# Groups of small matmuls ranked forty numbers ahead, and a norm's sums traced later, in a two-layer trunk

## The chip, the cores and the metric

The kernel runs on one core of one Trainium2 chip. The metric is the device time of one execution in microseconds. TensorE (PE in the profile, PEld for its weight loads) multiplies, VectorE (DVE) and ScalarE (ACT) do elementwise work, GpSimd (POOL) adds squares and clears tiles, SyncE (SP) issues the weight DMAs.

## The reference

A trunk of two layers on x of 512 tokens by 1024 features, all in fp32.

```python
for l in range(DEPTH):                       # DEPTH = 2
    h = rms_norm(x, attn_norm[l])
    if l % 2 == 0:  mix = hgrn_rwkv_mixer(h, ...)     # 4 HGRN heads, 8 RWKV heads, then @ w_out
    else:           mix = moba_mixer(h, ...)          # 8 attention heads, then @ w_o
    x = x + mix
    h = rms_norm(x, mlp_norm[l])
    x = x + square(relu(h @ w_up[l])) @ w_down[l]     # d_ff = 4096
    ple = rms_norm(p[l] @ ple_proj[l], ple_norm[l])   # p: the second input, 256 features
    x = x + ple * sigmoid(x @ ple_gate[l])
```

`rms_norm` divides by the root of the mean square over the features.

## The kernel before

Features lie on the partitions and the 512 tokens on the free axis, so x is eight tiles of 128 x 512. A large product (`gemm`, `mm3`, L243 to L259) splits weights and activations into a high part (fp32r) and a rest, and does three 512-column matmuls for each 128 x 128 block of weights (L244, L245, L246). Weights come in pieces of 128 x 512 (`wnext`): a DMA, ACT's cast to `whi` (L236), DVE's rest `wlo` (L237). The results stand in PSUM rings: `pj` and `pmh` with two banks each, `pmr` with four.

**Layer 0's mixer** has two streams of small work beside the large projections. The HGRN heads h = 0 to 3 (`hgrn`) use `pmh`. The RWKV head pairs (`pre`, `p1`, `p2`, `p3`, `tail`) use `pmr`. The small jobs are groups: four or so matmuls of 64 or 128 columns, or transposes, into one bank, which an evacuation follows. L664 (`half4`) are f16 groups of the inversion of a triangular matrix in `p2`, L519 (`four`) another, L710 and L711 are fp32 products of `p3`; an fp32 matmul shows as two passes in the trace. Steps are traced for each h in the order A F H B O C: A and C are runs of RWKV work, F the three projections of the HGRN head, H the HGRN head, B the projections of the next RWKV head, O an eighth of the output projection (`out_piece`). L803 is the first matmul group of an HGRN head and L896 its last.

**The order on each engine** is made when the program is built. Every traced instruction gets the next number. The scheduler plays the program through with its own costs and gives each engine, whenever it is free, the ready instruction with the lowest number. Each engine then works strictly in this order and waits for data where the scheduler was too early. `tc.high_priority(offset=n)` lowers the numbers inside by n; on leaving, the numbering goes on from where it was, so that instructions inside use up no numbers outside. `run` (L786) and the RWKV projections use `OFS` = 300. In the numbers of this program, head after head starts 314 later.

**The norms.** `NormAcc` (L306) squares each x tile on ACT (L313) and sums the squares on GpSimd (L319) into one tile `acc`, of which there is one buffer for all norms. `Stats.add` (L289) then sums over partitions by matmuls with ones (L291), `rs` takes the reciprocal root on DVE in 12 small steps (L300, L264 to L269), and `norm_rows` spreads the result over the partitions with transposes (L334) and an ACT copy (`rb`, L343). `later` (L1010) holds steps back: `flush` is called at each evacuation of the output projection of layer 1 and of the up products, and an entry of count n is traced at the (n+1)th call.

**Layer 0's MLP** gets its norm from code at the end (L1302): eight `add` calls, then `later_norm(st, 3, 1)`. **Layer 1's MLP** gets it inside `proj_out`: each evacuation adds to x (L1085), then `post` makes the scaled split (L280, L281) and traces the square and the sum; `later_norm(st, 2)` follows. **The second input** (`ple`, L1026) is projected, summed by its own `NormAcc`, and finished by `rows` (the root; L1047) and `finish` (transposes, then eight DVE steps, L1052). It is needed only in the gate after the MLP. In layer 1 `rows` comes at the 6th flush, in the output projection, and `finish` at the 9th, the first of the up product; in layer 0 `finish` comes at the 9th as well. The up products keep their PSUM banks until the norm's row is there: the first four use `pmr`, the next `pj`.

Of the kernel before, what the change touches and what calls it, by code (L numbers as in the profile page):

```python
# [12 lines left out]
F32 = mybir.dt.float32  # L13
# [16 lines left out]
FD = (3, 5)  # L30
# [4 lines left out]
OFS = 300  # L35
NWARM = 9
# [149 lines left out]
def trunk(ctx, tc, wts, xT, pT, vecs, lora, cst, lev, seg, rope, gain, out, upto="all", dbg=None, mode=None):  # L186
# [97 lines left out]
    class Stats:  # L284
# [4 lines left out]
        def add(self, sq, rhs):  # L289
            for j in range(NJ):  # L290
                T.matmul(self.ps[:, j * self.cols:(j + 1) * self.cols], sq[:, j * P:(j + 1) * P], rhs,  # L291
                         start=(self.i == 0 and j == 0), stop=(self.i == self.n - 1),
                         skip_group_check=True)
            self.i += 1
# [31 lines left out]
    def bcast_rows(rt, cols, pool, tag):  # L326
        ps = pool.tile([P, S], F32, name=tag)
        if cols > 1:
            full = nrm.tile([P, S], F32, name="bc")
            V.tensor_copy(full.rearrange("p (c w) -> p c w", w=P // cols),  # L330
                          rt[:, :, None].to_broadcast([P, NJ * cols, P // cols]))
        for j in range(NJ):
            lhs = full[:, j * P:(j + 1) * P] if cols > 1 else rt[:, j:j + 1].to_broadcast([P, P])
            T.transpose(ps[:, j * P:(j + 1) * P], lhs, ident)  # L334
        return ps
# [28 lines left out]
    def layer0_mixer(actp):  # L364
# [223 lines left out]
        def p1(hp, g):  # L588
            lw, bh, kh, ar, rh_, bo, dl, v, y = pre_[hp]
            gs = slice(g * 256, g * 256 + 256)  # L590
            NA, KA, TOK = NAs[g], KAs, []
            un[hp, g] = (NA, TOK)

            for n, (src, dst) in enumerate(((bh, NA), (kh, KA))):
                for h in range(2):
                    A.copy(BH[hs[h], n, :, hs[h]], src[hs[h], gs].rearrange("p (c t) -> p c t", t=64))
                ps = pmr.tile([P, S], F32, name="pmr")
                for c_ in range(4):
                    o = g * 256 + c_ * 64
                    T.matmul(ps[:, c_ * P:c_ * P + P].rearrange("p (x t) -> p x t", x=2), BH[:, n, c_, :],  # L600
                             ar[:, :, o:o + 64], start=True, stop=True)
                pv = ps.rearrange("p (a c x t) -> p a c x t", a=2, c=2, x=2)
                for h in range(2):
                    for c_ in range(2):
                        V.tensor_tensor(dst[hs[c_], :, h, :, hs[c_]], pv[hs[h], :, c_, :, :],
                                        tri[hs[h], None, :, :].to_broadcast([64, 2, 2, 64]), op=OP.mult)
                yield
            for a in range(2):
                j = 2 * g + a
                js = slice(j * P, j * P + P)  # L610

                ps = pmr.tile([P, S], F32, name="pmr")
                for n, src in enumerate((ar[:, 0, :], v, bh, kh)):
                    T.transpose(ps[:, n * P:n * P + P], src[:, js], ident)
# [9 lines left out]
            for i, (a, h) in enumerate(pk):  # L624
                T.matmul(ps[:, i * 64:i * 64 + 64], KA[:, a, h, 0, :], TOK[a][:, 1, hs[h]], start=True, stop=True)
# [4 lines left out]
            for i, (a, h) in enumerate(pk):  # L630
                T.matmul(ps[hs[h], a * P:a * P + P], TOK[a][:, 1, hs[h]], KA[:, a, h, 1, :], start=True, stop=True)
            A.copy(y[:, gs], ps[:, :256])
            yield

        def p2(hp, g):
# [11 lines left out]
            for l in range(1, 6):  # L647
# [27 lines left out]
            for i, (a, h) in enumerate(pk):  # L675
                T.matmul(ps[:, i * P:i * P + P], NA[:, a, h, 0, :], tt[:, i, :], start=True, stop=False)
                T.matmul(ps[:, i * P:i * P + P], id16, id16, start=False, stop=True)
# [4 lines left out]
            for i in range(4):  # L682
                T.matmul(ps[:, i * P:i * P + P], er[:, i, :], XT[:, i, :], start=True, stop=False)
                T.matmul(ps[:, i * P:i * P + P], id16, XT[:, i, :], start=False, stop=True)
# [4 lines left out]
            for i, (a, h) in enumerate(pk):  # L689
                T.matmul(ps[:, i * P:i * P + P].rearrange("p (x f) -> p x f", x=2), tt[:, i, :],  # L690
                         TOK[a][:, 0::2, hs[h]], start=True, stop=True)
# [6 lines left out]
        def p3(hp, g):  # L698
# [5 lines left out]
            for a in range(2):  # L704
# [3 lines left out]
                for c_ in range(2):  # L708
                    o = ps[:, 256 + c_ * P:256 + c_ * P + P]
                    T.matmul(o, bz[:, 0, c_, :], MU[:, a, 1, :], start=True, stop=False)  # L710
                    T.matmul(o, bz[:, 1, c_, :], TOK[a][:, 1, :], start=False, stop=True)  # L711
# [11 lines left out]
            def inner():  # L723
                ps = pmr.tile([P, S], F32, name="pmr")
                for i, (a, h) in enumerate(pk):
                    T.matmul(ps[hs[h], a * P:a * P + P], MU[:, a, 0, hs[h]], NA[:, a, h, 1, :], start=True, stop=True)
# [3 lines left out]
                for i, (a, h) in enumerate(pk):  # L730
                    T.matmul(ps[hs[h], a * P:a * P + P], MU[:, a, 1, hs[h]], NA[:, a, h, 1, :], start=True, stop=True)
# [20 lines left out]
            for c_ in range(f, 4):  # L752
                ch = 4 * g + c_
                T.matmul(ps[:, c_ * 64:c_ * 64 + 64], SB[:, ch, :], rh_[:, ch * 64:ch * 64 + 64], start=True, stop=True)
# [43 lines left out]
        def hgrn(h, q, ff, iv, gproj):  # L798
# [3 lines left out]
            for j in range(NJ):  # L802
                T.transpose(ps[:, j * P:j * P + P], iv[:, j * P:j * P + P], ident)  # L803
# [25 lines left out]
            for j in range(NJ):  # L829
                js = slice(j * P, j * P + P)  # L830
                T.matmul(ps[:, js], ks[:, js], d[:, js], start=True, stop=True)
            V.copy_predicated(at, m8[:, 13, None, :].to_broadcast([P, NJ, P]), j4(ps))
            for l in range(2, 7):
# [15 lines left out]
                for j in range(NJ):  # L849
                    js = slice(j * P, j * P + P)  # L850
                    T.matmul(ps[:, j * 64:j * 64 + 64], ks[:, js], qs[:, j * 64:j * 64 + 64], start=True, stop=True)
# [15 lines left out]
            for j in range(3):  # L867
                T.transpose(ps[:, j * P:j * P + P], d[:, j * P:j * P + P], ident)
# [3 lines left out]
            for j in range(3):  # L872
                T.matmul(ps[:, j * P:j * P + P], kt[:, j * P:j * P + P], vt[:, j, :], start=True, stop=True)
# [6 lines left out]
            for j in range(NJ):  # L880
                js = slice(j * P, j * P + P)
                T.matmul(ps[:, js], at[:, j, :], vt[:, j, :], start=True, stop=(j == 0))
                if j:
                    T.matmul(ps[:, js], q[:, js], st_[:, j * P - P:j * P], start=False, stop=True)
# [10 lines left out]
            for j in range(NJ):  # L895
                T.transpose(ps[:, j * P:j * P + P], ot[:, j * P:j * P + P], ident)  # L896
# [128 lines left out]

    def ple(l, plp):  # L1026
# [12 lines left out]
        def body():  # L1039
# [3 lines left out]
            later.append([FD[l] + 3, finish])  # L1043
# [303 lines left out]
```

## Time and profile before

| | us |
|---|---|
| median of 3 runs | 1511.21 |
| lowest and highest | 1510.91, 1512.28 |
| the profiled execution | 1511.89 |
| its span, first to last instruction | 1510.1 |
| TensorE busy in the span | 1478.1 |
| layer 0's mixer, from the start to the MLP | 0 to about 450 |
| layer 0's MLP and gate | about 450 to 865 |
| layer 1's attention | about 865 to 1089 |
| layer 1's output projection (second half) | 1086 to 1106 |
| layer 1's MLP and gate | 1106 to 1510 |

All times in the text are in microseconds from the first instruction of the profiled execution. A matmul's duration includes its way through the array, so the time that one costs TensorE is read from the start of one to the start of the next.

### The profile page before, as it was taken

The page shows a single profiled execution, that of the slowest core. Times are in us where ns is not written, and L with a number is a line of the kernel's source. Part 1 is how long each engine was busy: PE and PEld are TensorE (multiplying, and loading weights), DVE is VectorE, ACT ScalarE, POOL GpSimd, SP SyncE. Part 2 cuts the span into 40 slices and gives each one's busy share as a digit, 9 for nine tenths or more (in the row PEclk, how much of TensorE's full clock was granted, in tenths as well). Part 3 has the DMA queues.
Part 4 walks back from the last instruction along what each step waited for, and adds up shares of the span by engine and source line. Part 5 has one row for each costly group of instructions (what it writes and reads, how often), then busy time and mean ns, then how long its engine had stood idle before and what let it go on. Part 6 is the DMA issues. An engine that isn't in the chain of part 4 may idle for free.

```text
span 1510.1 us, 20495 instructions
## 1 busy us (share of the span) xinstructions
PE 1478.1 (98%) x7546; PEld 1191.3 (79%) x7546; DVE 937.6 (62%) x1835; ACT 663.1 (44%) x1269; POOL 138.4 (9%) x133
## 2 busy tenths in 40 slices
PE   8899999999989999999999999999999999999998
PEld 6678777777667888888888888777778888888887
DVE  6878797687785664444446648377575444445463
ACT  4675545554446433333334534455634333333342
POOL 4121220310205000000000200000220000000000
PEclk9999999999999999999999999999999999999999
DMA  5110111211123233333333432221123333333331
GB/s 179 56 36 22 55 50 39 66 29 47 39 91 106 90 98 98 98 98 98 98 95 98 124 118 84 77 63 50 56 80 95 95 101 98 98 96 93 98 98 70
DMA packets 67109, 123.88 MB, mean 82 GB/s; under 512 B 7632, under 2 KB 8016, under 8 KB 67008
## 3 DMA queue, kind: packets, MB, share of 16 engines
q1 hardware_dynamic: 65376, 118.57, 25.6%
q10 hardware_dynamic: 1152, 2.43, 0.5%
q0 software_dynamic: 480, 1.57, 0.3%
q8 instruction: 59, 0.97, 0.3%
q14 instruction: 42, 0.34, 0.1%
HBM read 120.45 MB, written 2.10 MB: 81 GB/s over the span
## 4 chain that ended last, share of the span: by engine, by line
PE 87%; DVE 7%; ACT 3%; issue 2%; DMA 1%; POOL 1%; SPq 0%; DVEq 0%; ACTq 0%; POOLq 0%
PE pj L244 20%; PE pj L246 20%; PE pj L245 20%; PE pmr L1273 1%; PE pmr L245 1%; PE pmr L1249 1%; PE pmr L246 1%; PE pmr L244 1%; PE pj L1176 1%; PE pmr L1176 1%; PE pj L1178 1%; PE pmr L1177 1%; PE pmr L1178 1%; PE pj L1177 1%; PE pmh L1176 1%
## 5 line engine op out<-in xcount | busy, mean ns | idle before, releaser
L236 ACT CAST whi<-wr 128x512 fp32r<-128x512 f32 x428 | 265.0, 621 | 549.2 <-PE pj L245 421.9
L237 DVE TENSOR_TENSOR wlo<-wr,whi 128x512 fp32r<-128x512 f32 x428 | 312.5, 733 | 197.6 <-ACT whi L236 193.6
L244 PE MATMUL pj<-act,whi 128*128 128x512 f32 (+1 forms) x856 | 338.1, 396 | 1.2 <-DVE h L935 1.0
L245 PE MATMUL pj<-act,whi 128*128 128x512 f32 (+1 forms) x856 | 336.8, 394 | 0.0
L246 PE MATMUL pj<-act,wlo 128*128 128x512 f32 (+1 forms) x856 | 335.7, 393 | 0.5 <-DVE wlo L237 0.5
L244 PE MATMUL pj<-hid,whi 128*128 128x512 f32 x512 | 199.2, 389 | 0.0
L245 PE MATMUL pj<-hid,whi 128*128 128x512 f32 x512 | 199.2, 389 | 0.0
L246 PE MATMUL pj<-hid,wlo 128*128 128x512 f32 x512 | 199.2, 389 | 0.0
L244 PEld LDWEIGHTS pj<-act,whi 128*128 128x128 f32 x856 | 161.1, 188 | 34.4 <-ACT k L491 1.4
L246 PEld LDWEIGHTS pj<-act,wlo 128*128 128x128 f32 x856 | 161.2, 188 | 32.5 <-DVE wlo L237 1.5
L245 PEld LDWEIGHTS pj<-act,whi 128*128 128x128 f32 x856 | 161.2, 188 | 31.1 <-issue 1.5
L1115 DVE TENSOR_TENSOR x<-x,pj 128x512 f32<-128x512 f32 x128 | 88.0, 688 | 80.6 <-PE pj L246 80.2
L245 PEld LDWEIGHTS pj<-hid,whi 128*128 128x128 f32 x512 | 96.1, 188 | 20.0
L244 PEld LDWEIGHTS pj<-hid,whi 128*128 128x128 f32 x512 | 96.1, 188 | 19.9
L246 PEld LDWEIGHTS pj<-hid,wlo 128*128 128x128 f32 x512 | 96.1, 188 | 19.9
L319 POOL TENSOR_TENSOR acc<-acc,xsq 128x512 f32<-128x512 f32 x35 | 48.7, 1393 | 628.8 <-ACT xsq L313 616.0
L1104 DVE SCALAR_TENSOR_TENSOR r<-pj,rb 128x512 f32<-128x512 f32 x56 | 38.7, 691 | 84.0 <-PE pj L246 84.0
L278 DVE TENSOR_TENSOR hid<-r,hid 128x512 fp32r<-128x512 f32 x64 | 44.3, 691 | 41.5 <-ACT hid L277 41.4
L1105 ACT ACTIVATE r<-r 128x512 f32<-128x512 f32 x64 | 40.5, 632 | 21.6 <-DVE r L1104 21.5
L277 ACT CAST hid<-r 128x512 fp32r<-128x512 f32 x64 | 39.8, 621 | 1.9
L280 ACT ACTIVATE act<-x,vec 128x512 fp32r<-128x512 f32 x32 | 22.9, 720 | 29.4 <-DVE x L1133 12.7
L244 PE MATMUL pj<-os,whi 128*128 128x512 f32 x64 | 28.3, 445 | 4.4 <-DVE x L946 2.8
(387 smaller groups left out, 2225.8 us busy)
## 6 DMA issues: line engine op xcount, KB each, us to landing
wr<-in_wts_dram SPq DMA_DIRECT2D x428, 256.0 KB, 2.7
x<-in_xT_dram SPq DMA_DIRECT2D x8, 256.0 KB, 6.3
sr<-in_wts_dram SPq DMA_DIRECT2D x8, 256.0 KB, 5.3
out_dram<-x SPq DMA_DIRECT2D x7, 256.0 KB, 2.0
r<-in_pT_dram ACTq DMA_DIRECT2D x4, 256.0 KB, 3.0
lw<-in_lora_dram POOLq DMA_DIRECT2D x4, 192.0 KB, 3.1
tq<-in_rope_dram ACTq DMA_DIRECT2D x1, 512.0 KB, 6.7
tk<-in_rope_dram ACTq DMA_DIRECT2D x1, 512.0 KB, 7.6
```

The lines of the kernel that those rows point to most:

```text
L236: A.copy(hi, raw)
L237: V.tensor_sub(lo, raw, hi.bitcast(F32))
L244: T.matmul(ps, wh, xh, start=first, stop=False)
L245: T.matmul(ps, wh, xl, start=False, stop=False)
L246: T.matmul(ps, wl, xh, start=False, stop=last)
L277: A.copy(h, src)
L278: V.tensor_sub(l, src, h.bitcast(F32))
L319: G.tensor_add(self.t, self.t, sq)
L1104: V.scalar_tensor_tensor(r, q, 0.0, nf[0], op0=OP.max, op1=OP.mult)
L1105: A.activation(r, r, AF.Square)
L1115: V.tensor_add(x[k], x[k], ps)
L1176: T.matmul(ps[j], xh, wh, start=k == 0, stop=False)
```

## The change

A context `tight()` is `tc.high_priority(offset=40)`. It is put around the small groups: in `Stats.add`, in `bcast_rows`, and at 20 places in the mixer, of which two are shown. DVE's, ACT's and GpSimd's instructions are not inside it. Layer 1's MLP norm is taken out of `proj_out` into `rows_norm`, which layer 0 uses too, and `finish` moves by six flushes in both layers.

```diff
+TIGHT = 40
+    def tight():
+        return tc.high_priority(offset=TIGHT)
     class Stats:
         def add(self, sq, rhs):
-            for j in range(NJ):
-                T.matmul(...)
+            with tight():
+                for j in range(NJ):
+                    T.matmul(...)
     def bcast_rows(rt, cols, pool, tag):
-        for j in range(NJ):
-            T.transpose(...)
+        with tight():
+            for j in range(NJ):
+                T.transpose(...)
         def four(lhs, rhs):
             ps = pmr.tile([P, S], F32, name="pmr")
-            for i in range(4):
-                T.matmul(ps[:, i * P:i * P + P], lhs(i), rhs(i), start=True, stop=True)
+            with tight():
+                for i in range(4):
+                    T.matmul(ps[:, i * P:i * P + P], lhs(i), rhs(i), start=True, stop=True)
...
                 def half4(lhs, rhs):
-                    for i in range(4):
-                        T.matmul(pv[:, i], lhs[:, i, :], rhs[:, i], start=True, stop=True)
+                    with tight():
+                        for i in range(4):
+                            T.matmul(pv[:, i], lhs[:, i, :], rhs[:, i], start=True, stop=True)
...
+    def rows_norm():
+        st = NormAcc(lambda: tmp.tile([P, S], F32, name="xsq"))
+        for k in range(8):
+            st.add(x[k])
+        return later_norm(st, 3, 1)
     def ple(l, plp):
             later.append([FD[l], rows])
-            later.append([FD[l] + 3, finish])
+            later.append([FD[l] + 9, finish])
     def proj_out(name, acts, l):
-        st, xg = NormAcc(lambda: tmp.tile([P, S], F32, name="xsq")), []
+        xg = []
                 V.tensor_add(x[k], x[k], ps)
-                post(k, st, act, "act", vcol(f"mn{l}", k), xg)
+                xg.append(split(act, x[k], "act", vcol(f"mn{l}", k)))
-        return st, xg
+        return xg
...
-        st = NormAcc(lambda: tmp.tile([P, S], F32, name="xsq"))
-        for k in range(8):
-            st.add(x[k])
-        nf = later_norm(st, ND[0] + 1, 1)
+        nf = rows_norm()
...
-        st, xg = proj_out("o", o, 1)
-        xs = mlp(1, later_norm(st, ND[1]), xg)
+        xg = proj_out("o", o, 1)
+        xs = mlp(1, rows_norm(), xg)
```

## Rows read from the trace of the kernel before

**Rows 1.** Part 1 of the page: busy time, share of the span, instructions.

```profile
PE 1478.1 (98%) x7546; PEld 1191.3 (79%) x7546; DVE 937.6 (62%) x1835; ACT 663.1 (44%) x1269; POOL 138.4 (9%) x133
```

**Rows 2.** Stretches: bounds, length, busy of PE PEld DVE ACT POOL, clock, DMA.

```profile
20.00:385.00 365.00, 353.27 (x2429) 277.64 (x2427) 278.68 (x658) 194.53 (x435) 64.34 (x68) 1.00 0.15 46
385.00:440.00 55.00, 47.73 (x313) 36.69 (x313) 44.88 (x106) 25.46 (x52) 11.01 (x9) 0.99 0.21 63
455.00:490.00 35.00, 33.05 (x149) 26.37 (x148) 19.40 (x30) 20.51 (x37) 19.33 (x14) 1.00 0.37 114
1106.00:1131.00 25.00, 23.04 (x92) 18.02 (x91) 18.55 (x40) 7.89 (x14) 4.76 (x4) 0.86 0.25 74
```

**Rows 3.** Two more stretches of the same view.

```profile
600.00:640.00 40.00, 40.00 (x178) 33.15 (x177) 19.86 (x30) 13.90 (x23) 0.00 (x0) 1.00 0.30 94
1114.95:1121.70 6.75, 6.75 (x20) 5.54 (x20) 6.07 (x11) 0.57 (x1) 0.00 (x0) 0.50 0.25 78
```

**Rows 4.** Timeline of TensorE: start, duration, engine, line, operation, tiles, shapes, count.

```profile
165.31 0.20 PE L664 MATMUL pmr<-PP,XT 128*128 128x64 f16 x1
...
386.95 0.20 PE L664 MATMUL pmr<-XT,PP 128*128 128x64 f16 x1
386.99 0.47 PE L246 MATMUL pj<-act,wlo 128*128 128x512 f32 x1
387.31 0.20 PE L664 MATMUL pmr<-XT,PP 128*128 128x64 f16 x1
```

**Rows 5.** Timeline of TensorE where two groups stand whole.

```profile
317.45 0.29 PE L664 MATMUL pmr<-PP,XT 128*128 128x64 f16 x4
317.57 0.28 PE L664 MATMUL pmr<-XT,PP 128*128 128x64 f16 x4
```

**Rows 6.** Timeline of TensorE, fp32 pairs.

```profile
169.29 0.38 PE L710 MATMUL pmr<-MU,BZ 128*128 128x128 f32 x2
...
169.75 0.38 PE L711 MATMUL pmr<-TOK,BZ 128*128 128x128 f32 x2
```

**Rows 7.** Timeline of TensorE at layer 1's output projection and MLP start.

```profile
1099.38 0.95 PE L291 MATMUL pmh<-ones,acc 128*128 128x1 f32 x8
...
1112.65 0.50 PE L244 MATMUL pmr<-act,whi 128*128 128x512 f32 x1 [1.52 <-ACT act L280]
```

**Rows 8.** Timelines of GpSimd and TensorE at layer 0's MLP start.

```profile
453.91 10.69 POOL L319 TENSOR_TENSOR acc<-acc,xsq 128x512 f32<-128x512 f32 x7 [16.93 <-ACT xsq L313]
...
464.66 1.05 PE L291 MATMUL pmh<-ones,acc 128*128 128x1 f32 x8 [0.77 <-POOL acc L319]
```

**Rows 9.** Timelines of GpSimd, ACT and DVE at layer 1's MLP start.

```profile
1083.80 6.07 POOL L319 TENSOR_TENSOR acc<-acc,xsq 128x512 f32<-128x512 f32 x4
...
1101.13 8.51 POOL L319 TENSOR_TENSOR acc<-acc,xsq 128x512 f32<-128x512 f32 x6 [11.26 <-ACT acc L313]
...
1100.36 0.63 ACT L313 ACTIVATE acc<-x 128x512 f32<-128x512 f32 x1 [0.39 <-PE pmh L291]
...
1101.64 1.33 DVE L281 SCALAR_TENSOR_TENSOR act<-x,vec,act 128x512 fp32r<-128x512 f32 x1 [0.37 <-ACT act L280]
...
1104.38 1.15 DVE L268 SCALAR_TENSOR_TENSOR ra_n<-ra_n,m_n 128x4 f32<-128x4 f32 x1
...
1105.64 0.68 DVE L1085 TENSOR_TENSOR x<-x,pj 128x512 f32<-128x512 f32 x1
...
1111.16 0.68 DVE L1085 TENSOR_TENSOR x<-x,pj 128x512 f32<-128x512 f32 x1
```

**Rows 10.** Timeline of DVE at layer 0's `finish`.

```profile
539.55 5.35 DVE L1052 SCALAR_TENSOR_TENSOR ple<-ple,vec,pmh 128x512 f32<-128x512 f32 x8
```

**Rows 11.** Lines L803, L896 (min/median/max ns, first to last start); stretch, pmr alone.

```profile
L803 PE MATMUL pmh<-cs,h x16: 270/272/273, 80.1 to 389.9; 128*128 128x128 f32 x16
...
L896 PE MATMUL pmh<-cs,h x16: 271/273/329, 159.8 to 431.4; 128*128 128x128 f32 x16
...
390.00:432.00 42.00, 15.17 (x126) 9.63 (x82) 8.90 (x24) 4.97 (x14) 1.00 0.14 43
```

More of the change, by code (lines that the diff above doesn't have):

```diff
@@ L623, in p1 @@
             ps = pmr.tile([P, S], F32, name="pmr")
-            for i, (a, h) in enumerate(pk):
-                T.matmul(ps[:, i * 64:i * 64 + 64], KA[:, a, h, 0, :], TOK[a][:, 1, hs[h]], start=True, stop=True)
+            with tight():
+                for i, (a, h) in enumerate(pk):
+                    T.matmul(ps[:, i * 64:i * 64 + 64], KA[:, a, h, 0, :], TOK[a][:, 1, hs[h]], start=True, stop=True)
             for a in range(2):
@@ L629, in p1 @@
             ps = pmr.tile([P, S], F32, name="pmr")
-            for i, (a, h) in enumerate(pk):
-                T.matmul(ps[hs[h], a * P:a * P + P], TOK[a][:, 1, hs[h]], KA[:, a, h, 1, :], start=True, stop=True)
+            with tight():
+                for i, (a, h) in enumerate(pk):
+                    T.matmul(ps[hs[h], a * P:a * P + P], TOK[a][:, 1, hs[h]], KA[:, a, h, 1, :], start=True, stop=True)
             A.copy(y[:, gs], ps[:, :256])
@@ L681, in p2 @@
             ps = pmr.tile([P, S], F32, name="pmr")
-            for i in range(4):
-                T.matmul(ps[:, i * P:i * P + P], er[:, i, :], XT[:, i, :], start=True, stop=False)
-                T.matmul(ps[:, i * P:i * P + P], id16, XT[:, i, :], start=False, stop=True)
+            with tight():
+                for i in range(4):
+                    T.matmul(ps[:, i * P:i * P + P], er[:, i, :], XT[:, i, :], start=True, stop=False)
+                    T.matmul(ps[:, i * P:i * P + P], id16, XT[:, i, :], start=False, stop=True)
             A.copy(tt, ps.rearrange("p (i t) -> p i t", i=4))
@@ L707, in p3 @@
                 T.matmul(ps[:, :256], MU[:, a, 0, :], bz[:, 0].rearrange("p c f -> p (c f)"), start=True, stop=True)
[L708 to L711, printed above, removed]
+                with tight():
+                    for c_ in range(2):
+                        o = ps[:, 256 + c_ * P:256 + c_ * P + P]
+                        T.matmul(o, bz[:, 0, c_, :], MU[:, a, 1, :], start=True, stop=False)
+                        T.matmul(o, bz[:, 1, c_, :], TOK[a][:, 1, :], start=False, stop=True)
                 pv = ps.rearrange("p (x c f) -> p x c f", x=2, c=2)
@@ L724, in inner @@
                 ps = pmr.tile([P, S], F32, name="pmr")
[L725 to L726 removed]
+                with tight():
+                    for i, (a, h) in enumerate(pk):
+                        T.matmul(ps[hs[h], a * P:a * P + P], MU[:, a, 0, hs[h]], NA[:, a, h, 1, :], start=True, stop=True)
                 V.tensor_add(rh_[:, gs], rh_[:, gs], ps[:, :256])
@@ L729, in inner @@
                 ps = pmr.tile([P, S], F32, name="pmr")
-                for i, (a, h) in enumerate(pk):
-                    T.matmul(ps[hs[h], a * P:a * P + P], MU[:, a, 1, hs[h]], NA[:, a, h, 1, :], start=True, stop=True)
+                with tight():
+                    for i, (a, h) in enumerate(pk):
+                        T.matmul(ps[hs[h], a * P:a * P + P], MU[:, a, 1, hs[h]], NA[:, a, h, 1, :], start=True, stop=True)
                 V.tensor_add(y[:, gs], y[:, gs], ps[:, :256])
@@ L751, in p3 @@
             f = 1 if g == 0 else 0
-            for c_ in range(f, 4):
-                ch = 4 * g + c_
-                T.matmul(ps[:, c_ * 64:c_ * 64 + 64], SB[:, ch, :], rh_[:, ch * 64:ch * 64 + 64], start=True, stop=True)
+            with tight():
+                for c_ in range(f, 4):
+                    ch = 4 * g + c_
+                    T.matmul(ps[:, c_ * 64:c_ * 64 + 64], SB[:, ch, :], rh_[:, ch * 64:ch * 64 + 64], start=True, stop=True)
             yg = y[:, g * 256 + f * 64:g * 256 + 256]
@@ L828, in hgrn @@
             ps = pmh.tile([P, S], F32, name="pmh")
-            for j in range(NJ):
-                js = slice(j * P, j * P + P)
-                T.matmul(ps[:, js], ks[:, js], d[:, js], start=True, stop=True)
+            with tight():
+                for j in range(NJ):
+                    js = slice(j * P, j * P + P)
+                    T.matmul(ps[:, js], ks[:, js], d[:, js], start=True, stop=True)
             V.copy_predicated(at, m8[:, 13, None, :].to_broadcast([P, NJ, P]), j4(ps))
@@ L848, in hgrn @@
                 ps = pmh.tile([P, S], F32, name="pmh")
-                for j in range(NJ):
-                    js = slice(j * P, j * P + P)
-                    T.matmul(ps[:, j * 64:j * 64 + 64], ks[:, js], qs[:, j * 64:j * 64 + 64], start=True, stop=True)
+                with tight():
+                    for j in range(NJ):
+                        js = slice(j * P, j * P + P)
+                        T.matmul(ps[:, j * 64:j * 64 + 64], ks[:, js], qs[:, j * 64:j * 64 + 64], start=True, stop=True)
                 def hi(t):
@@ L871, in hgrn @@
             ps = pmh.tile([P, S], F32, name="pmh")
-            for j in range(3):
-                T.matmul(ps[:, j * P:j * P + P], kt[:, j * P:j * P + P], vt[:, j, :], start=True, stop=True)
+            with tight():
+                for j in range(3):
+                    T.matmul(ps[:, j * P:j * P + P], kt[:, j * P:j * P + P], vt[:, j, :], start=True, stop=True)
             st_ = Hh()
@@ L879, in hgrn @@
             ps = pmh.tile([P, S], F32, name="pmh")
[L880 to L884, printed above, removed]
+            with tight():
+                for j in range(NJ):
+                    js = slice(j * P, j * P + P)
+                    T.matmul(ps[:, js], at[:, j, :], vt[:, j, :], start=True, stop=(j == 0))
+                    if j:
+                        T.matmul(ps[:, js], q[:, js], st_[:, j * P - P:j * P], start=False, stop=True)
             sq = Hh()
```

53 lines of the change are left out of this document (30 added, 23 removed).

## The prediction

> **What bounds the kernel now.** I read the page's busy times first: TensorE works 1478 of 1510 us [rows 1], so a change can win only what TensorE idles, what it spends on switching between kinds of matmul, and what it runs at half clock. The table by stretches shows where the idle time lies [rows 2]: 365.00 - 353.27 = 11.7 us between 20 and 385 us (layer 0's mixer), 7.3 us in the mixer's last 55 us, 1.95 us at layer 0's MLP start (455 to 490) and 1.96 us at layer 1's (1106 to 1131), where the granted clock is also below full. The MLP itself leaves nothing: in 600:640 it is busy for all 40.00 us, one 512-column matmul each 40/178 = 0.225 us [rows 3]. So the change acts in the mixer and at the two MLP starts; the other 1000 us stay.
>
> **Part 1, `tight()` in the mixer.** No instruction is added or removed, no DMA moves, and no queue but TensorE's is reordered directly. The cost of a cut group is read in TensorE's timeline at 387 us [rows 4]: a 64-column f16 matmul (L664) starts at 386.95, one projection matmul at 386.99, the next L664 at 387.31, so small and large together take 0.36 us. Where the four stand together, they take 317.57 - 317.45 = 0.12 us, 0.03 each [rows 5], and a large one 0.225: 0.255. A cut therefore costs 0.105 us. I counted groups over the whole timeline: 52 times exactly one large matmul stands inside a group, from 165.31 to 387.31 us [rows 4], 37 of them in f16 groups (31 of L664, 6 of L519), 15 in fp32 groups (12 of L710/L711, 3 of L731). For an fp32 pair the rows give 169.75 - 169.29 = 0.46 us with its large matmul [rows 6]; two passes at the 0.95/8 = 0.12 of L291 [rows 7] and 0.225 make 0.465, so these cost nothing.
>
> The cause is rank. Head h's C run starts at 1145 for h = 3 and its numbers then equal those of F(3)'s projections, which start near 1130: two streams are merged one to one. After the change a group ranks 40 earlier, and since numbers are given back on leaving `tight()`, the run's later numbers fall behind by 4 for each group too; the hgrn head loses 45 of the 314 numbers from one head to the next, so 269 are left, under the offset of 300, and C(3) starts some 31 ahead of F(3). Groups then go out whole as soon as they are ready. **Gain 37 x 0.105 = 3.9 us.** Other cuts (22 more, ended by waiting for data) I leave: they are a matter of readiness. Bounds of the reorder itself: the 11.7 us of idle in 20:385 may go or double, since a group at the head of TensorE's queue holds all behind it; I take 0, because the run's groups rank first at most places already.
>
> **Part 2, the statistics at layer 0's MLP.** `Stats.add` is `tight` too. L291 of the MLP norm waits in TensorE's queue for GpSimd's seven sums, which end at 453.91 + 10.69 = 464.60; it starts at 464.66 after 0.77 us of idle [rows 8]. It stood just behind the second up tile in rank. Forty numbers are 34 large matmuls, and in the program's order of issue the last sum stands 16 matmuls ahead of L291, the sums themselves about 5 apart. So the scheduler takes the sums for done some 10 matmuls earlier than the trace shows, and puts L291 there. Queued behind it are the second up tile's last products and the ple projection, and DVE and ACT wait on those. **Cost 10 x 0.225 = 2.2 us**, between 0 (later readiness) and 34 x 0.225 = 7.7 us (no readiness limit). At layer 1's attention norm the early place falls about where the last sum ends: between 0 and one more such wait of 0.77, **0.2 us** taken, since sums there come one by one and none queues. The norm's broadcast (L334) is also earlier, but its input is long there: nothing.
>
> **Part 3, layer 1's MLP start.** TensorE stops at 1112.65 for 1.52 us, waiting for ACT's scaled copy of x7 [rows 7], 1.96 us in all [rows 2], and the clock is then 0.50, the 1.2 GHz level, from 1114.95 to 1121.70 [rows 3]; that stretch holds half the work, so at most 3.4 us are lost, and I take 3.2 since a few waits lie inside. Together 5.2 us. Why is x7 late? DVE adds it at 1111.16 with no wait before it, so it was late by its own queue [rows 9]: ahead stood the ple norm's reciprocal root, whose four-element steps take 1.15 us (L268 at 1104.38) while GpSimd sums squares from 1101.13 to 1109.64 [rows 9]. That block begins at 1100.36, when ACT may write the single `acc` buffer, because the ple norm's L291 read it only at 1099.38 [rows 7]. With `tight` that L291 ranks 40 earlier, 24 matmuls or 5.7 us, to about 1093.7, when its sums have ended (1083.80 + 6.07 = 1089.87) [rows 9]. The root and the x sums then start 5.7 us earlier, spread over projection tiles that come each 2.7 us, and ACT does squares after the copies. **Gain 5.2 us, less 0.3** if L291 of the MLP norm meets its last sum as now: 4.9. Bounds: one more such stop, 1.96 us lost, to 5.2 gained.
>
> `finish` moves from the 9th flush to the 15th. Its eight DVE steps take 5.3 us in one piece [rows 10]; before, the MLP norm's first DVE step stood behind them, after, they lie between up tiles. Two pj buffers give DVE one tile, 24 x 0.225 = 5.4 us, to empty a bank; 5.3 and one 0.7 us step would overrun by 0.6 us at most, and layer 0's finish at 539 us [rows 10] makes TensorE lose nothing: 0. The norm's rows come one tile later; four pmr buffers and two pj cover 6 tiles, 32 us: 0.
>
> The Trainium skill's page "SBUF — State Buffer", section "Who interferes with whom", speaks against part 3: a DVE instruction with two SBUF inputs contends with a GpSimd instruction that reads SBUF, and the loser is blocked for the whole instruction, while one with at most one SBUF input is not. The trace agrees: L268, two SBUF inputs, took 1.15 us beside the sums; L1085 at 1105.64, with one operand in PSUM, 0.68 [rows 9]. By that rule moving the sums moves the blocking along: that is rival 1.
>
> **Sum.** Profiled execution 1511.9 (span 1510.1): -3.9 + 2.2 + 0.2 - 4.9 = -6.4, 1505.5. The median of the runs is 0.7 below that execution: **1505 us**.
>
> **Rivals.**
> 1. *The blocking moves along.* DVE's two-input steps (L281, L237) meet the sums beside the projection, x5 to x7 come late, and TensorE stops as now. For it: L281 took 1.33 us at 1101.64, beside the sums [rows 9]. Against: spread over six tiles, DVE meets one sum at a time. 1505 + 4.9 = 1510.
> 2. *Slower: the filler is used up early.* hgrn head 3 runs as one chain from L803 at 389.9 to L896 at 431.4, 41.5 us, and out_piece(3) waits for its `os` [rows 11]. What fills TensorE beside it is head 3's RWKV work, 15.2 us on pmr banks [rows 11]. If this ranks ahead of F(3), F(3) and the whole chain end later by what is moved. At 12 us (the tail's own products stay) the time is 1505 + 12 = 1517; from 9 us on the kernel is slower. For it: the ranks above. Against: TensorE is full until 385, and DVE, 44.9 of 55 us busy there [rows 2], would be freer for the chain.
> 3. *The mixer's end gains.* With RWKV done earlier head 3 has DVE and ACT to itself, and the 7.3 us of idle in 385:440 go: 1498.
> 4. *Groups stay cut*, because they are held by their data and not by rank: the 3.9 us don't come: 1509.
> 5. *L291 at layer 0 is put 34 matmuls early*, 7.7 us in place of 2.2, and the clock falls as it did after the 1.96 us of layer 1: 1512.
>
> **How the numbers follow.** Forecast 0.44, rivals 1 to 5: 0.14, 0.18, 0.13, 0.06, 0.05. About 3 us (0.2%) is what a measurement of this kernel can tell from no change, so 1508.2 to 1514.2 is the same. Faster: forecast and rival 3, 0.57; same: rivals 1, 4, 5, 0.25; slower: rival 2, 0.18. The range goes from rival 3 less 1 us to where 11 us of rival 2 have moved: 1497 to 1516.
>
> **What would show it.** Right: no single L664 between projection matmuls at 165 to 388 us; layer 1's ple L291 near 1094 minus the mixer's gain, x7 added within 1 us of its projection, no clock of 0.50 there; at layer 0 TensorE idle about 3 us before L291. Wrong: L803 of head 3 later than 390 us (rival 2), or x7 still 5 us late (rival 1). The stretches 490:822 and 1131:1510 must not change by more than 0.5 us.

## The result, and the profile after

The kernel before took 1511.06 us, the changed one **1535.47 us** (medians of four runs each, in pairs on one chip): the ratio is 1.0154, with a 95% interval of 1.0135 to 1.0174. The forecast was 1505, the range 1497 to 1516. The profiled execution of the changed kernel has a span of 1533.2 us, 23.1 more than before.

In the code after, the lines stand lower: L244 to L246 are now L249 to L251, L291 is L297, L664 is L677, L803 is L824, L896 is L923, L1085 is L1118. First part 1 of the page after, then the stretches that answer to [rows 2], in the same columns, and one more at half clock.

```profile
PE 1489.8 (97%) x7546; PEld 1203.0 (78%) x7546; DVE 935.4 (61%) x1835; ACT 664.5 (43%) x1269; POOL 137.6 (9%) x133
```

```profile
20.00:385.00 365.00, 350.57 (x2360) 277.48 (x2358) 272.17 (x646) 191.03 (x428) 63.50 (x67) 0.99 0.14 43
385.00:440.00 55.00, 50.32 (x319) 39.91 (x319) 35.41 (x82) 22.58 (x46) 10.00 (x9) 0.94 0.14 39
455.00:490.00 35.00, 28.33 (x109) 21.47 (x109) 23.64 (x40) 17.29 (x30) 11.44 (x8) 0.90 0.25 74
1106.00:1131.00 25.00, 22.97 (x103) 18.15 (x102) 21.37 (x34) 16.46 (x29) 13.55 (x10) 1.00 0.32 93
226.30:229.70 3.40, 3.40 (x14) 2.25 (x14) 1.38 (x2) 0.34 (x1) 0.19 (x1) 0.50 0.21 77
```

TensorE has the same 7546 instructions, but is busy for 11.7 us more, and idles 43.4 us in place of 32.0. Two things in these rows were not in the forecast: the granted clock is 0.50 from 226.3 to 229.7 in the middle of the mixer, where it was full before, and in the first 385 us TensorE gets through fewer instructions (2360, 2429 before) though it is hardly less busy. So in that stretch most of the time is lost in the matmuls themselves (it idles 14.4 us, 11.7 before); of the whole 23.1 us about half is busy time and half idle.

**Where it is lost**, by equal work: I gave each matmul the step that its shape usually takes from start to start (large 0.224 us, an fp32 pass of 64 or 128 columns 0.111, f16 of 64 columns 0.029, of 128 columns 0.056) and read in both timelines when the same sum of steps was done. These are the differences to the kernel before in us, at six of its times (a kernel's start alone moves by up to 1.8: so much at 20 us); the other kernels come below. Each row is one execution, and e8_rwkv's took 4 us more than the median of its runs, e9_cols2's 2.7 less.

| kernel | 283 | 373 | 452 (mixer's end) | 506 (MLP's up) | 983 (attention) | 1196 (layer 1's MLP) |
|---|---|---|---|---|---|---|
| the change | +9.9 | +17.1 | +19.6 | +23.2 | +24.1 | +23.1 |
| e1_mixer | +9.8 | +16.2 | +20.1 | +20.0 | +20.0 | +19.8 |
| e2_norms | -3.2 | -3.2 | -4.8 | -1.2 | -0.4 | +0.2 |
| e3_keep | -1.1 | -0.6 | -4.4 | -0.8 | +0.2 | -0.9 |
| e4_zero | +19.5 | +25.4 | +25.2 | +25.2 | +25.1 | +22.0 |
| e6_keep345 | -1.1 | -1.4 | +1.1 | +5.8 | +6.7 | +5.6 |
| e7_hgrn | -1.1 | -1.3 | +0.8 | +5.2 | +6.1 | +6.7 |
| e8_rwkv | +4.0 | +6.6 | +10.3 | +15.0 | +15.8 | +14.7 |
| e15_rwkv345 | +4.9 | +8.4 | +8.4 | +12.9 | +13.8 | +12.6 |
| e11_back200 | +9.5 | +18.4 | +17.8 | +21.4 | +22.2 | +21.1 |
| e12_cols255 | +3.9 | +4.7 | +5.7 | +7.4 | +7.4 | +5.6 |
| e9_cols2 | -1.6 | -1.0 | -5.7 | -5.7 | -5.7 | -7.5 |
| e10_mixkeep | -0.3 | +0.3 | -4.7 | -4.7 | -4.8 | -4.5 |
| e13_root | -2.1 | -1.5 | -6.6 | -6.7 | -6.8 | -8.6 |
| e14_dep | -0.9 | -0.4 | -5.4 | -5.5 | -5.6 | -10.7 |

The change loses 17 us while TensorE is still full (up to 373), 2.5 at the mixer's end, 3.6 at layer 0's MLP start, 0.9 at the attention norm, and wins 1.0 back in layer 1.

**What is lost in the mixer.** Counted over TensorE's order up to the mixer's end. The added time is what the steps take over the usual ones; single steps with over 0.15 us extra are waits and stand by themselves, from 0.35 on in the last column but one. Steps that start at half clock are in the last column alone, with all that they took extra.

| kernel | single f16 between two large, from 165 us | f16 and fp32 as neighbours | added, a large matmul at one side | added among small ones | waits over 0.35 | lost at half clock |
|---|---|---|---|---|---|---|
| before | 47 | 165 | 17.2 | 6.9 | 29.2 | 1.4 |
| the change | 0 | 318 | 12.9 | 19.5 | 35.6 | 8.5 |
| e3_keep | 0 | 163 | 12.5 | 5.9 | 31.6 | 3.5 |

The first and third number columns are part 1 of the prediction as it was meant: no f16 matmul stands alone between two projections any more, and that brings 4.3 us. The fourth shows the price: 12.6 us more among the small matmuls, and 6.4 and 7.1 in waits and at half clock (2.1 come back in waits of 0.15 to 0.35; together 19.7). Here is one fp32 group of `p3` (L731 before, L750 after), whose products go into one half of the partitions each (128*64 in the row), in TensorE's timeline (start, duration, engine, line, operation, tiles, shapes, count), first in the kernel before, then in the changed one.

```profile
316.86 0.66 PE L731 MATMUL pmr<-NA,MU 128*64 128x128 f32 x8
317.45 0.23 PE L664 MATMUL pmr<-PP,XT 128*128 128x64 f16 x2
```

```profile
327.58 0.43 PE L750 MATMUL pmr<-NA,MU 128*64 128x128 f32 x2
327.95 0.20 PE L677 MATMUL pmr<-PP,XT 128*128 128x64 f16 x1
...
328.25 0.43 PE L750 MATMUL pmr<-NA,MU 128*64 128x128 f32 x2
328.62 0.20 PE L677 MATMUL pmr<-PP,XT 128*128 128x64 f16 x1
...
328.81 0.43 PE L750 MATMUL pmr<-NA,MU 128*64 128x128 f32 x2
329.17 0.20 PE L677 MATMUL pmr<-XT,PP 128*128 128x64 f16 x1
```

Before, all eight passes stand together and the next instruction starts 0.59 us later, 0.15 for each two passes. After, f16 matmuls of the inversion (L677) stand between them, and two passes take 0.37, 0.37 and 0.36 us: 0.22 more each time. It is the cut that costs, not the f16 neighbour: in both kernels such a run of two passes takes 0.36 or 0.37 us whatever follows it, a large matmul too. The 192 passes of this kind stand in 34 runs before, 19 of them whole eights, and in 65 after, 4 of them eights; from the first pass of each run to the instruction behind it they take 16.9 us before and 25.3 after. These 8.4 us are two thirds of the 12.6; the step of a small matmul just ahead of such a run is 0.09 us longer too, some 2.9 us more by an estimate from the 31 further ones. The f16 neighbours of full-width fp32 products cost little (from the changed kernel's timeline):

```profile
225.44 0.44 PE L690 MATMUL pmr<-tt,NA 128*128 128x128 f32 x2
225.72 0.22 PE L691 MATMUL pmr<-id 128*128 128x128 f16 x1
```

Here two passes take 0.28 us with an f16 matmul ahead and behind, 0.06 over the usual.

### The profile page after: what moved, and what is told of

Its sections match the earlier page's. It is cut to its first block, busy times and chain, and to the rows that moved or that the text cites. A ratio compares the mean times of both kernels' runs of the same rounds, so it can differ in the third digit from the quotient of the medians.

```text
span 1533.2 us, 20498 instructions
## 1 busy us (share of the span) xinstructions
PE 1489.8 (97%) x7546; PEld 1203.0 (78%) x7546; DVE 935.4 (61%) x1835; ACT 664.5 (43%) x1269; POOL 137.6 (9%) x133
## 4 chain that ended last, share of the span: by engine, by line
PE 66%; DVE 1%; ACT 1%; POOL 1%; issue 1%; POOLq 0%; ACTq 0%; DVEq 0%
PE pj L249 17%; PE pj L250 17%; PE pj L251 17%; PE pmr L1306 1%; PE pmr L1282 1%; PE pj L1209 1%; PE pj L1211 1%; PE pj L1210 1%; PE pmh L1209 1%; PE pmh L1211 1%; PE pmh L1210 1%; PE pmr L1211 1%; PE pmr L1209 1%; PE pmr L1210 1%; PE pmr L251 1%; PE pmr L249 1%
## 5 line engine op out<-in xcount | busy, mean ns | idle before, releaser
L238 DVE TENSOR_TENSOR wlo<-wr,whi 128x512 fp32r<-128x512 f32 x428 | 310.2, 727 | 198.6 <-ACT whi L237 196.2
L249 PE MATMUL pj<-act,whi 128*128 128x512 f32 (+1 forms) x856 | 336.0, 394 | 2.1 <-DVE x L1118 1.9
L251 PE MATMUL pj<-act,wlo 128*128 128x512 f32 (+1 forms) x856 | 336.1, 394 | 0.7 <-DVE wlo L238 0.7
L249 PE MATMUL pj<-hid,whi 128*128 128x512 f32 x512 | 199.5, 390 | 0.0
L251 PE MATMUL pj<-hid,wlo 128*128 128x512 f32 x512 | 199.5, 390 | 0.0
L249 PEld LDWEIGHTS pj<-act,whi 128*128 128x128 f32 x856 | 161.0, 188 | 36.9 <-DVE x L1118 3.3
L251 PEld LDWEIGHTS pj<-act,wlo 128*128 128x128 f32 x856 | 161.1, 188 | 34.1 <-DVE wlo L238 2.0
L251 PEld LDWEIGHTS pj<-hid,wlo 128*128 128x128 f32 x512 | 96.2, 188 | 20.0
L249 PEld LDWEIGHTS pj<-hid,whi 128*128 128x128 f32 x512 | 96.2, 188 | 19.9
L250 PEld LDWEIGHTS pj<-hid,whi 128*128 128x128 f32 x512 | 96.2, 188 | 19.7
L249 PE MATMUL pj<-os,whi 128*128 128x512 f32 x64 | 27.6, 434 | 5.7 <-DVE x L973 3.8
```

Of the source, the lines that this page charges most:

```text
L238: V.tensor_sub(lo, raw, hi.bitcast(F32))
```

## Experiments

**e1 and e2: each half alone.** e1_mixer keeps only the 20 `tight()` places of the mixer, e2_norms only the rest.

> Only part 1: tight() at the 20 places of the mixer; Stats.add, bcast_rows, layer 1's norm and finish as before. From the trace of the changed kernel, by equal work done, 19.6 of its 23.1 us are there by the mixer's end, 3.5 more come at layer 0's MLP start and layer 1 nets nothing. If the mixer's order is the cause, this kernel takes 1511 + 19.6 = 1531 us (1528 to 1533). If layer 0's statistics, placed early, are the root and the mixer only shifted with them, it stays near 1511.

Measured 1530.05 us, ratio 1.0116 (1.0090 to 1.0142). The mixer's order is 19 of the 24 us, and these need nothing from the norms.

> Only parts 2 and 3: Stats.add and bcast_rows tight, layer 1's norm traced behind the output projection, finish six flushes later; the mixer's 20 places as before. If the parts add up: 1511 + 3.5 (wait of the statistics at layer 0's MLP and the half clock behind it) + 0.9 (attention norm) - 1.2 (layer 1's MLP start) = 1514 (1511 to 1517). By the prediction's own terms (2.2 + 0.2 - 4.9) it would be 1508.5.

Measured 1512.73, ratio 1.0008 (0.9999 to 1.0017). The parts don't quite add up: the trace is 3.2 us ahead at 283, of which 1.6 are there at 20 us, as a kernel's start moves; where the rest comes from is open. The two norms take 3.6 and 0.8 of it back.

**e3 and e4: rank against numbers.** `tight()` does two things: it lowers a group's numbers by 40, and it gives them back, so that the next instruction is numbered as if the group weren't there. e3_keep does the first alone, e4_zero the second alone.

```diff
 e3_keep
+    @contextmanager
     def tight():
-        return tc.high_priority(offset=TIGHT)
+        p = tc.cur_priority
+        with tc.high_priority(offset=TIGHT):
+            yield
+            p += tc.cur_priority - (p - TIGHT)
+        tc.cur_priority = p
...
 e4_zero
-TIGHT = 40
+TIGHT = 0
```

> As the changed kernel, but tight() lowers a group's numbers by 40 and then goes on behind them, so that its instructions use up numbers as before. Theory A: groups that use up no numbers have numbers that overlap those of the next group of the same run, so groups of two jobs are merged one to one (12.6 us of added time between small matmuls, and half clock and idle behind it); then this kernel keeps the gain of whole groups (about 4 us) and loses the rest: 1511 - 4 + 3 = 1510 (1504 to 1516). Theory B: it is the rank, 40 ahead, that lets RWKV work go before the projections and leaves hgrn head 3 without filler; then this kernel is as slow as the changed one, 1530 or more.

> As the changed kernel, but with an offset of 0 in tight(): the groups' numbers are not lowered, only given back. Theory A: the mixer's merged groups stay, so the mixer loses about what it lost, while the statistics are early no more: 1511 + 19.6 - 1 = 1530 (1524 to 1535). Theory B: without the lower rank the mixer is as before: 1511 (1508 to 1515).

Measured: e3_keep 1512.31 us, 1.0007 (0.9998 to 1.0017); e4_zero 1536.45 us, 1.0163 (1.0138 to 1.0188). With the kernel before and the change these are all four corners, but for the later norm, which the kernel before lacks and which e9 and e10 below find worth nothing that can be told: **given back or not makes 23 to 25 us**. 40 ahead or not makes 1 us in the sum, because two effects cancel: by the table it wins 4.4 and 5.6 us up to the mixer's end and loses 4.6 and 4.5 at the two norms behind it. Groups of one run whose instructions use up no numbers overlap in number with the next groups, and when both are ready the scheduler takes them one by one in turn, as the rows of L750 and L677 show. The third row of the table above, e3_keep's, agrees: neighbours of both types are back at 163, the added time among small ones at 5.9, and the 4 us of part 1 are there (-4.4 at the mixer's end).

**e6, e7, e11, e12: the run's rank, rival 2.** What moves C(3) ahead of F(3) without any merging is a larger OFS (e6_keep345: e3_keep with 345) or the HGRN head's give-back alone (e7_hgrn: 7 groups of the head give back, 13 of RWKV keep). e11_back200 is the changed kernel with OFS 200.

> As e3_keep (groups 40 ahead, numbers used up as before), with OFS 345 in place of 300. This sets the RWKV runs 45 numbers further ahead, which is what the hgrn head's lost numbers do to the run C(3) in the changed kernel: it stands ahead of F(3)'s projections, and hgrn head 3 comes behind it. Groups are not merged. Rival 2 of the prediction (filler used up early, a price of 12 us): 1512 + 12 = 1524, with head 3's first matmul later than 400 us. Merging alone (theory A): 1512 to 1516, since by equal work the changed kernel lost only 2.5 us in its last 60 us of the mixer.

> As e3_keep, but the 7 groups of the HGRN head give their numbers back as in the changed kernel; the 13 of the RWKV jobs keep them. e8_rwkv (the other way round) is 10 us slower than e3_keep, the changed kernel 23. If the HGRN groups' own give-back only moves the run C(3) ahead of F(3), this kernel is like e6_keep345: 1516 (1513 to 1519), with head 3's first matmul near 396. If it costs the remaining 13 us by itself, 1525 (1522 to 1529). If it costs only together with the RWKV groups (both then rank alike and merge with each other), 1516 too, and the rest is an effect of both.

> As the changed kernel, but OFS 200 in place of 300: numbers are given back and groups merge as there, but the RWKV runs rank 100 later, so C(3) no longer stands ahead of F(3). Rival 2 alone (filler used up early): the loss goes, 1511 to 1516. Merging: only the 6 us go that the changed kernel lost against e3_keep in the mixer's last 60 us; 1535 - 6 = 1529 (1524 to 1534).

Measured: e6_keep345 1516.43, 1.0030 (1.0019 to 1.0041); e7_hgrn 1518.08, 1.0039 (1.0025 to 1.0052); e11_back200 1532.93, 1.0142 (1.0126 to 1.0157). The first matmuls of the HGRN heads (min/median/max ns, first to last start), in e3_keep, then e6_keep345, then the change:

```profile
L828 PE MATMUL pmh<-cs,h x16: 270/272/302, 71.9 to 386.2; 128*128 128x128 f32 x16
```

```profile
L828 PE MATMUL pmh<-cs,h x16: 270/272/303, 72.2 to 397.6; 128*128 128x128 f32 x16
```

```profile
L824 PE MATMUL pmh<-cs,h x16: 270/273/330, 70.5 to 418.2; 128*128 128x128 f32 x16
```

With the rank alone head 3 starts 11 us later, and TensorE has 3.2 us more idle in the stretch of its chain (44.77 busy of 55, 47.96 in e3_keep) at a clock of 0.94:

```profile
385.00:440.00 55.00, 44.77 (x243) 35.18 (x241) 39.26 (x93) 24.32 (x49) 10.61 (x9) 0.94 0.22 72
```

```profile
385.00:440.00 55.00, 47.96 (x301) 37.13 (x301) 45.54 (x106) 26.07 (x54) 11.03 (x9) 0.97 0.23 68
```

So rival 2 is real, but worth 4 to 6 us by the runs (6.5 and 7.6 by the traces), not 12. In the change, head 3 starts 28 us later than before [rows 11], but 17 of these had been lost before. e11_back200 undoes the rank and leaves the merging: 2.5 us come back, and 18 us are still lost at 373. The 100 numbers are more than the 45 to be undone, and a later rank can cost by itself (e12 below), so the 2.5 are no clean price of the rank.

> As e9_cols2 (1507.1), but OFS 255 in place of 300: the opposite step to e6_keep345, which was 4 us slower than e3_keep. If the RWKV work's rank against F(3) sets the mixer's end, this is faster than e9_cols2 by up to 4: 1503 to 1507. If 300 is already late enough, RWKV work that comes later leaves the chains of A and C longer: 1507 to 1511.

e12_cols255 took 1515.80, 1.0032 (1.0020 to 1.0043), slower by 9 than e9_cols2 below. The granted clock was 0.50 for 24 us of its mixer, from 121.3 and from 404.6 us, and in the table's count 12.6 us were lost there, against 2.1 in e9_cols2: nearly all of the 11.4 between them at the mixer's end. What let it fall is open. A rank later than that of 300 doesn't pay either.

**e8 and e15: whose numbers.** e8_rwkv: the 13 RWKV groups give back, the 7 of the HGRN head keep. e15_rwkv345: the same with OFS 345.

> As e3_keep, but the 13 groups of the RWKV jobs give their numbers back as in the changed kernel; the 7 of the HGRN head keep them. Theory A: RWKV jobs woven into one run merge with each other, so the mixer's loss is there: 1512 + 19 = 1531 (1525 to 1536). If the 45 numbers that the HGRN head loses are the cause, it is away: 1512 (1509 to 1516).

> As e8_rwkv (RWKV groups give their numbers back, HGRN groups keep them; 1522.6), with OFS 345: to the merging RWKV groups comes the rank shift of 45 that the HGRN groups' give-back makes in the changed kernel (1535.5), without that give-back itself. If the shift on top of merging is the changed kernel's other 13 us: 1532 to 1537. If the HGRN groups' own merging with RWKV groups is: 1521 to 1526.

Measured: e8_rwkv 1522.61, 1.0070 (1.0055 to 1.0085); e15_rwkv345 1526.16, 1.0098 (1.0083 to 1.0113). Neither expectation of e8 was met: the RWKV groups' give-back costs 10 us over e3_keep, not 19, and the rank shift on top 3.5 by the runs (the traces can't tell, as said above the table); e15 lies at the top of the range for the HGRN groups' own merging. The change's other 9 us come only when the HGRN groups give back too, which cost nothing of the kind alone (e7_hgrn at 373: -1.3). By the traces a good part of it is half clock: the change has two stretches of 3.41 us at 0.50 in mid-mixer, at 226 and 335 us, with 4.2 us of added time, of which the clock can hold at most 3.4 (half of 2 x 3.41); neither e8 nor e15 has one between 20 and 400. Up to the mixer's end, against e15's trace, the change has 5.3 us more at half clock, 3.5 in long waits and 3.2 among small matmuls. Ahead of the first stretch, the changed kernel's TensorE had had only small matmuls since 222.48 and stood 1.42 us for ACT:

```profile
223.22 0.41 PE L774 MATMUL pmr<-ar,SB 128*128 128x64 f32 x2
225.06 0.49 PE L690 MATMUL pmr<-tt,NA 128*128 128x128 f32 x2 [1.42 <-ACT tt L686]
```

Why it takes both give-backs is open. That the two streams' groups merge with each other, as e15's expectation had it, is not borne out: a small matmul on pmh stands beside one on pmr 43 times in the change, 41 in e8, 42 in e15 and 72 before.

**e9 and e10: the statistics and the later norm.** e9_cols2 is e3_keep with `Stats.add` tight only for the two-column statistics of the mixer; e10_mixkeep has layer 1's norm and `finish` as before too.

```diff
         def add(self, sq, rhs):
-            with tight():
+            with tight() if self.cols > 1 else nullcontext():
```

> As e3_keep, but Stats.add is tight only where it has two columns (the mixer's statistics), and not for the norms and the second input. By e3_keep's trace the early statistics cost 3.6 us at layer 0's MLP start and 0.9 at layer 1's attention norm, and layer 1's MLP start still has a wait of 2.4 us for the last sum. If these waits come from the early place of the statistics, they go: 1512 - 4.5 - 1 = 1507 (1504 to 1511). If they come from the later tracing of the sums, layer 1's wait stays: 1508 to 1509.

> As e9_cols2, but with layer 1's norm and finish traced where the kernel before has them. The mixer alone: the gain that the prediction gave part 1, 3.9 us, of which e3_keep's trace shows 4.4 by equal work at the mixer's end: 1511 - 4 = 1507 (1505 to 1511). The difference to e9_cols2 is what the later norm is worth by itself: by the prediction a gain of 4.9 us less for e9_cols2; if the ple norm's early statistics were what was to bring it, no difference.

Measured: e9_cols2 **1507.10**, 0.9963 (0.9951 to 0.9976); e10_mixkeep 1507.28, 0.9973 (0.9963 to 0.9984). Both beat the kernel before, by the mixer's 4 to 5 us; the later norm alone makes no difference that these runs can tell. L297 in the changed kernel's timeline, at layer 0's MLP norm, the attention norm and layer 1's MLP norm (in brackets the idle time ahead of it and who ended it), and at layer 0 in e9_cols2 (L301):

```profile
484.17 1.05 PE L297 MATMUL pmh<-ones,acc 128*128 128x1 f32 x8 [3.66 <-POOL acc L325]
...
888.76 1.05 PE L297 MATMUL pmh<-ones,acc 128*128 128x1 f32 x8 [0.70 <-POOL acc L325]
...
1138.40 0.38 PE L297 MATMUL pmh<-ones,acc 128*128 128x1 f32 x2 [2.27 <-POOL acc L325]
```

```profile
458.96 1.05 PE L301 MATMUL pmh<-ones,acc 128*128 128x1 f32 x8 [0.77 <-POOL acc L329]
```

Without `tight` the 3.66 us are 0.77 again, as in [rows 8], the attention norm's wait is gone, and so is layer 1's. Nor does `tight` keep L297 whole: ranked 40 ahead it lands among projection matmuls, and is taken in turn with them. The second input's, in the changed kernel, stands in pieces:

```profile
1117.36 0.28 PE L297 MATMUL pmh<-ones,acc 128*128 128x1 f32 x2
1117.50 0.48 PE L251 MATMUL pj<-act,wlo 128*128 128x512 f32 x1
1117.81 0.28 PE L297 MATMUL pmh<-ones,acc 128*128 128x1 f32 x2
1117.95 0.47 PE L249 MATMUL pj<-act,whi 128*128 128x512 f32 x1
```

And e10 shows one more: with the norm traced early and its broadcast tight, TensorE stands for the reciprocal root (L345 is the broadcast, L334 before).

```profile
1105.86 0.67 PE L345 MATMUL pmh<-cs,rs_n 128*128 128x128 f32 x4 [4.65 <-DVE rs_n L1078]
```

**e13 and e14: what makes x7 late.** Both are e9_cols2 with layer 1's reciprocal root of the second input's norm at a later flush; e14_dep also ties it to the MLP norm's root (`R["n"]`), which it takes in times zero.

```diff
-            rt.append(st.rs("n"))
-            V.tensor_scalar(rt[0], rt[0], 0.5, None, op0=OP.mult)
+            s2 = Stats(pmh, "pmh")
+            s2.add(st.t, ones)
...
+            V.tensor_scalar(m, s2.ps[:, :NJ], 1.0 / D, EPS, op0=OP.mult, op1=OP.add)
...
+            def root():
+                if l:                                          # e14_dep alone
+                    V.scalar_tensor_tensor(m, R["n"], 0.0, m, op0=OP.mult, op1=OP.add)
+                rt.append(rsqrt(m, NJ, "p"))
+                V.tensor_scalar(rt[0], rt[0], 0.5, None, op0=OP.mult)
+            if l:
+                later.append([6, root])
...
```

> As e9_cols2 (1507.1), but in layer 1 the reciprocal root of the second input's norm (eleven DVE steps of four elements, up to 1.25 us each beside GpSimd's sums) is traced at the 13th flush, between up tiles, in place of the 6th, in the output projection. e9_cols2's trace has x7's tile added 5.5 us after the one before it, TensorE idle 1.53 + 0.29 us for it, and the granted clock at 0.50 for 3.4 us behind that (half of which is lost). If the root's steps beside the sums make x7 late, as part 3 of the prediction had it, both go: 1507.1 - 1.8 - 1.7 = 1503.5 (1502 to 1506), x7 added within 3 us of x6, no 0.50 clock there. If the sums themselves (with the two-input steps that make the split's rest) do it, nothing changes: 1507 (1505 to 1509).

> As e9_cols2 (1507.1; e13_root 1504.2, where the root stayed where it was on VectorE though traced later): layer 1's root of the second input's norm takes in the MLP norm's root, times zero, so it can't start before it (one more DVE step of four elements). If the root's steps beside GpSimd's sums make x7 late, x7 is added within 3 us of x6, TensorE's 1.52 + 0.28 us of idle and the stretch at 0.50 behind it (1.7 us lost) go: e9_cols2 less 3.5, 1501 to 1504. If the sums with the two-input steps of the split do it, x7 stays 5 us behind x6 and the time is that of e9_cols2 and e13_root, 1504 to 1508.

Measured: e13_root 1504.15, 0.9958 (0.9944 to 0.9971); e14_dep **1501.33**, 0.9935 (0.9921 to 0.9950), the fastest kernel of this study. One step of the root and the add of x7's tile on DVE, then TensorE at x7, in e13_root and in e14_dep:

```profile
1097.58 1.15 DVE L277 SCALAR_TENSOR_TENSOR ra_p<-ra_p,m_p 128x4 f32<-128x4 f32 x1
...
1104.35 0.68 DVE L1132 TENSOR_TENSOR x<-x,pj 128x512 f32<-128x512 f32 x1
...
1105.84 0.50 PE L253 MATMUL pmr<-act,whi 128*128 128x512 f32 x1 [1.52 <-ACT act L289]
```

```profile
1101.25 0.75 DVE L290 SCALAR_TENSOR_TENSOR act<-x,vec,act 128x512 fp32r<-128x512 f32 x1 [2.87 <-ACT act L289]
...
1103.63 0.67 DVE L1139 TENSOR_TENSOR x<-x,pj 128x512 f32<-128x512 f32 x1
...
1117.33 0.15 DVE L277 SCALAR_TENSOR_TENSOR ra_p<-ra_p,m_p 128x4 f32<-128x4 f32 x1
...
1106.12 0.50 PE L254 MATMUL pmr<-act,whi 128*128 128x512 f32 x1 [0.51 <-DVE act L290]
```

In e13_root the root didn't move: traced seven flushes later (at the 13th in place of the 6th), it still ran at 1094 to 1104 beside the sums: the scheduler gives a free engine what is ready, however high its number, when nothing lower is. Its likeness to e9_cols2 says nothing on the cause. With the dependency the root runs behind the MLP norm's, a step takes 0.15 in place of 1.15 us, TensorE stands 0.51 in place of 1.52 and 0.28, and no clock of 0.50 follows: 5.1 us from 983 to 1196, of which 1.8 were e9's. So the root beside the sums costs some 3.3 us here, as part 3 had it: x7 is added at 1103.63 in place of e9's 1105.44, with x5 at 1094.29 and 1094.13. But x7 is still added 5.9 us behind x6, and 5 us was the expectation's sign of the sums: DVE waits 2.87 us for ACT's scaled copy (L289), which stands behind squares that GpSimd's sums hold back. Root and sums both make x7 late; without the root TensorE hardly stops for it.

## Why the prediction was wrong

- **Part 1, the reorder taken as 0: the step that failed.** The gain of whole groups was right in mechanism and size (37 x 0.105 = 3.9; 4.3 by the steps, 4.4 in e3_keep). I had read that groups use up no numbers, and used it only for the distance of run and projections. The same fact makes the groups of one run overlap in number, so that they cut each other: with the numbers used up (e3_keep) 23 us go. I priced a cut by a large matmul only, and took an fp32 pair's cut as free from full-width pairs [rows 6], L731 among them; a run of two passes of L731 takes 0.36 us where eight take 0.59, and the further cuts of such products cost 8.4 us. In place of 0 the term was 17.7 us, by the sum below. The bounds of the reorder, all or twice the 11.7 us of idle time, were bounds of waits: the loss was mostly in busy time, 12.6 us among small matmuls and 7.1 at half clock against 4.3 in waits.
- **Rival 2** had the right place, head 3's late start, and the wrong size: 12 us were forecast, 6.5 measured by the trace where it is alone (e6_keep345). Its chance of 0.18 was for the sign, and its ground (the rank) carries a quarter of the loss.
- **Part 2** was forecast at 2.2 us (0 to 7.7) and measured at 3.6: L297 starts after 3.66 us of idle time in place of 0.77, and the clock is 0.50 from 485.7 to 489.1, which only rival 5 had. The attention norm took 0.9, over its bound of 0.77.
- **Part 3**: forecast -4.9, measured -1.0. The 0.50 clock and x7's stop went, as forecast, and the second input's L297 came when it was worked out to: 1117.36 less the 24.3 lost ahead of it is 1093.1, forecast 1093.7 (1094.0 by 24 x 0.225 = 5.4 us, where the prediction had 5.7). But in the projection TensorE then stopped for 0.62 and 1.27 us for x tiles, since the blocking had moved along with the sums (rival 1), and L297 of the MLP norm, early too, stood 2.27 us for its last sum. The table's e14_dep shows the whole gain of about 5 us, from another edit.
- **`finish`** cost nothing, as forecast; the broadcast, also taken at nothing, costs 4.65 us where the norm is traced early (e10_mixkeep).
- **What would show it**: no single f16 between projections, right; L803 later than 390, the sign of rival 2, right; layer 0's MLP start, right; x7 within 1 us of its projection, wrong (2.3 us: the last projection matmul ends at 1132.74, DVE adds at 1134.99, behind the rest of a weight piece, L238, that took 1.44 us beside a sum); the long stretch of layer 1's MLP unchanged, right (busy 375.16 of 379 us, 375.03 before).

Put together, as an account and not a measurement of each term: merging 17.7 (the change against e3_keep at 373), rank 6.3 (what these two come further apart up to the mixer's end; 5.5 for the rank alone in e6_keep345), less 4.4 from whole groups, 3.6 and 0.9 for the early statistics, less 1.0 in layer 1: 23.1.

## What to carry to other kernels

Before an offset is put around a group, ask what number the *next* group gets: a context that gives its numbers back lets neighbours be taken in turn, and a lower rank is only safe if groups still follow one another in number. Count who stands beside whom on the engine, by kind of matmul, and price every kind of cut from the trace, small by small as well as small by large, and products into part of the array by themselves. A step that is to run later needs a dependency; a later place in the trace is only a wish.

## What the runs showed of the hardware

- fp32 products into the two halves of the partitions took 0.59 us for eight passes where they stood together, and 0.36 or 0.37 for two, whether an f16, a large or another fp32 matmul came next.
- DVE steps of four elements took 0.15 to 0.17 us alone and up to 1.25 beside GpSimd's sums, and the two-input step of the split 1.78 in place of 0.75 (L286, the changed kernel):

```profile
1112.98 1.78 DVE L286 SCALAR_TENSOR_TENSOR act<-x,vec,act 128x512 fp32r<-128x512 f32 x1
...
1116.49 0.74 DVE L286 SCALAR_TENSOR_TENSOR act<-x,vec,act 128x512 fp32r<-128x512 f32 x1
```

  The Trainium skill's page "SBUF — State Buffer", section "Who interferes with whom", states that a DVE instruction with two SBUF inputs contends with a GpSimd instruction that reads SBUF; these rows agree, and e14_dep shows what it was worth here. That a DVE instruction with at most one SBUF input does not contend, this page of the Trainium skill states only outside the 2-port perf modes, an exception that the prediction left out: L265, with one SBUF input, took 1.25 us at 1102.90 in the kernel before, beside the sums, and the same step (L274 in e14_dep) 0.16 at 1114.04 without them. Whether it runs in such a mode no run here shows.
